# Second layer's norm from sums taken before the residual add, ten row tiles held for the second tokens, and DVE's order tied through both chains

## The chip, the cores and the metric

The kernel runs on one core of a Trainium2 chip. The metric is device microseconds (us) for one execution. Engines are named as in the profile: PE is TensorE's matmul (PEld its weight load), DVE is VectorE, ACT is ScalarE, POOL is GpSimd, SP is SyncE, whose queue issues most of the DMAs.

## The reference

The kernel computes two layers over 256 tokens of width 2048. In each, the input is normed, modulated, projected by one wide weight matrix, sent through four attention branches and a gate, projected back, normed again and added to the input:

```
def rmsnorm(x, g):
    y = x * rsqrt(mean(x * x, axis=-1) + 1e-6)
    return y * g

for li in range(2):
    shift, scale, gate = split(silu(c) @ w_ada[li] + b_ada[li], 3)
    h = rmsnorm(x, g_pre[li]) * (1 + scale) + shift
    p = split_columns(h @ w_in[li])
    ...                                   # four branches, each 512 wide
    mixed = concat(branches) * silu(p["gate"])
    y = mixed @ w_out[li]
    x = x + gate * rmsnorm(y, g_post[li])
```

What matters here is the seam between the layers: `rmsnorm(y)` and the add give x, and the second layer's `rmsnorm(x, g_pre[1])` needs the sum of squares of each row of that new x. With r the reciprocal root of y's mean square and u = y * gate * g_post, the new row is x + r * u, and its sum of squares can also be had as sum(x^2) + r * sum(2*u*x) + r^2 * sum(u^2).

## The kernel before, in words

All of it is one function, `trunk`, with nested helpers; the instructions are written in program order, and a planner puts them in order on each engine when the kernel is built. The planner goes by a model of durations and gives a free engine the earliest instruction in program order among those that the model says are ready. On the chip each engine then follows that fixed order. `with tc.issue_after(ins)` keeps the instructions in it behind `ins` on their engine; it sets an order and waits for no data.

Tokens are two tiles t of 128 rows (T = 2), the width is 16 tiles kt of 128 (KT), and weights come two kt at a time (a unit k2). Products are made of two parts per operand: `split` (L297) has ACT round a weight unit to `whi` (L300) and DVE subtract for `wlo` (L301), and notes that subtraction as `ada.behind`; `mm3` (L318) issues three matmuls, L320 to L322. `weights` (L304) loads a unit on SP's queue (L310), splits it, and after every second unit calls `ada.run`, which sums weights of the modulation vectors that were loaded before (L143 on DVE, one pass over 128x1024 each with an accumulated output) and loads further ones (L133).

`tok_major` (L333) is a projection with tokens as rows. With `late` set, the last `late` of the 16 kt are multiplied for t = 0 only, held, and multiplied for t = 1 at the end, so that the result of t = 0 is ready earlier. Held units must keep their split weights: the last three have buffers of their own (`own`, L948 to L954), others stay in the three rotating pairs `whi`/`wlo` of the pool splp (L73).

The output projection (L943) has four column parts n of 512. For each and each t, ACT squares the result with an accumulated sum (L960) and DVE multiplies it by the gate row into `yg` (L961). In the last part (n = 3, late = 6) there follows, per t: the sum of the four parts (L966), mean and epsilon (L96), the power -1/2 on POOL (L97), four updates of x in place on DVE (L971), in the last layer four output DMAs (L973). In the first layer `norm_row` (L394) then squares the new x on ACT in four pieces (L399), sums (L401), takes L96 and L97 again, and `rms_row` scales the identity by the result (L429), has PE multiply it with ones (L431) to lay it out as a row, and ACT copies it to `rrow` (L432). x goes to DRAM (L979). Before the second token tile's `norm_row`, `turned` (L434) is written, in which PE transposes x for the first three units (L440).

The second layer begins with `ada.until(1, 3)` (L826), which has the outstanding L143 sums done up to its fourth unit, and with `modulated` (L443): per kt, DVE multiplies the transposed x by gain and `rrow` (L454), ACT adds the shift and rounds (L456), DVE takes the rest (L457). Then the first projections, `latent` (L369), split their weights and run.

x itself is loaded for the residual at L937, after the buffers of the mixed branches come free. `wk` is a rotating pool of four scratch tiles, `bank()` one of four PSUM banks.

Of the kernel before, what the change touches and what calls it, by code (L numbers as in the profile page):

```python
# [20 lines left out]
P = 128  # L21
D = 2048
# [31 lines left out]
LATE = 6  # L54
# [7 lines left out]
def trunk(ctx: ExitStack, tc: tile.TileContext, a):  # L62
# [31 lines left out]
    def rsqrt_mean(out, ssq, n, w):  # L94
        ms = small.tile([P, 8], F32, name="ms")
        nc.vector.tensor_scalar(ms[:, :w], ssq, 1.0 / n, EPS, op0=ALU.mult, op1=ALU.add)  # L96
        nc.gpsimd.tensor_tensor(out, ms[:, :w], mhalf[:, :w], op=ALU.pow)  # L97

# [23 lines left out]
    class Ada:  # L122
# [60 lines left out]
        def finish(self, L, li, u):  # L183
# [4 lines left out]
            else:  # L188

                h, j = (u - K2) // 2, (u - K2) % 2  # L190
                if j == 0:
                    self.gate = small.tile([P, 32], F32, name="gcol", bufs=2)
                    nc.gpsimd.memset(self.gate, 0.0)
# [4 lines left out]
                if j == 1:  # L198

                    turn = small.tile([P, 32], F32, name="grow", bufs=2)  # L200
                    nc.vector.transpose(turn, self.gate)
                    L.row[h] = row = dram.tile([8, 4, 32], F32, name=f"row{li}{h}")
                    for q in range(4):
                        nc.gpsimd.dma_start(row[:, q, :], turn[32 * q:32 * q + 8, :])
# [89 lines left out]
    def bank():  # L294
        return psm.tile([P, 512], F32, name="main")
# [98 lines left out]
    def norm_row(L, t):  # L394

        ssp = small.tile([P, 4], F32, name="ssp")
        jk = bank()
        for h in range(4):
            nc.scalar.activation(jk, L.cols(t, 512 * h, 512), AF.Square, accum_out=ssp[:, h:h + 1])  # L399
        ss = small.tile([P, 1], F32, name="ss")  # L400
        nc.vector.tensor_reduce(ss, ssp, axis=AX.X, op=ALU.add)  # L401
        rms_row(L, t, ss)

# [19 lines left out]
    def rms_row(L, t, ss):  # L423
        rstd = small.tile([P, 1], F32, name="rstd")
        rsqrt_mean(rstd, ss, D, 1)
        if t == 0:
            L.rrow = lay.tile([P, S], F32, name="rrow")
        dg = work.tile([P, 512], F32, name="wk")[:, 0:P]
        nc.vector.tensor_scalar(dg, ident, rstd, None, op0=ALU.mult)  # L429
        rp = bank()[:, 0:P]  # L430
        nc.tensor.matmul(rp, ones, dg, start=True, stop=True)  # L431
        nc.scalar.copy(L.rrow[:, t * P:(t + 1) * P], rp)  # L432

# [388 lines left out]
    def layer(li):  # L822
# [118 lines left out]
        ssy = small.tile([P, T, 4], F32, name="ssy", bufs=1)  # L941
        ygs = []
        for n in range(4):  # L943
# [14 lines left out]
            for t in range(T):  # L958
                jk = work.tile([P, 512], F32, name="wk")
                nc.scalar.activation(jk, ps[t], AF.Square, accum_out=ssy[:, t, n:n + 1])  # L960
                nc.vector.tensor_mul(yg[:, t, :], ps[t], gg[n // 2][:, 512 * (n % 2):512 * (n % 2) + 512])  # L961
                if n < 3:
                    continue
                ss = small.tile([P, 1], F32, name="ss")
                rstd = small.tile([P, 1], F32, name="rstd")
                nc.vector.tensor_reduce(ss, ssy[:, t, :], axis=AX.X, op=ALU.add)  # L966
                rsqrt_mean(rstd, ss, D, 1)
                for m in range(4):
                    cs = slice(512 * m, 512 * (m + 1))
                    xs = x[t][m // 2][:, 512 * (m % 2):512 * (m % 2) + 512]  # L970
                    nc.vector.scalar_tensor_tensor(xs, ygs[m][:, t, :], rstd, xs, op0=ALU.mult, op1=ALU.add)  # L971
                    if last:
                        nc.sync.dma_start(a["out"][t * P:(t + 1) * P, cs], xs)  # L973
                if not last:
                    if t == 1:
                        layers[li + 1].tp = [turned(layers[li + 1], k2) for k2 in range(3)]
                    norm_row(layers[li + 1], t)
# [113 lines left out]
```

## Time and profile before

| what | us |
|---|---|
| median of 3 runs | 1119.47 (1119.19 to 1120.66) |
| the profiled execution | 1120.7 |
| its span in the profile | 1118.9 |
| PE busy (matmul) | 1073.8 |
| DVE busy | 876.2 |
| ACT busy | 558.2 |
| POOL busy | 50.1 |

The span is the time between the first and the last instruction of the profiled execution; 1.8 us lie around it. Busy times of the engines overlap each other. Matmuls are pipelined, so that a matmul's listed duration is longer than the distance to the next one.

### The profile page before, as it was taken

The numbers are of one execution on the slowest core, as the hardware profiler recorded it, in microseconds if no ns is written. First come the engines' busy times: TensorE is split into PE (matmuls) and PEld (weight loads), VectorE is DVE, ScalarE is ACT, GpSimd is POOL, SyncE is SP. The second block draws the span as 40 slices with busy tenths as digits, with TensorE's granted clock in tenths as the row PEclk, the third lists the DMA queues.
The fourth block names the chain that finished last, engine by engine and source line by source line (L and its number), as shares of the span: only waits on it lengthen the run. The fifth ranks groups of instructions, "written<-read, shape, count | busy, mean of one in ns | idle before, by whom it ended". The sixth has DMA issues, their size and how long they took to land.

```text
span 1118.9 us, 19443 instructions
## 1 busy us (share of the span) xinstructions
PE 1073.8 (96%) x7562; PEld 991.2 (89%) x7562; DVE 876.2 (78%) x1470; ACT 558.2 (50%) x929; POOL 50.1 (4%) x70
## 2 busy tenths in 40 slices
PE   3899999999999999999959999999999999999996
PEld 2798989999899999988749999999999899998885
DVE  4598897999999778887778887989997655556463
ACT  3455344345454766654444554554554476645451
POOL 1000000000003000000000000000112000000000
PEclk9899999999999999999979999999999999999999
DMA  9998998988677677899867999867687765357541
GB/s 366 348 330 306 354 341 260 346 276 278 236 231 244 212 246 251 280 359 310 304 273 263 367 339 325 294 219 229 205 273 254 258 196 166 132 189 263 188 151 75
DMA packets 83308, 294.75 MB, mean 263 GB/s; under 512 B 9768, under 2 KB 10048, under 8 KB 83088
## 3 DMA queue, kind: packets, MB, share of 16 engines
q1 hardware_dynamic: 81216, 288.36, 74.5%
q0 software_dynamic: 1856, 5.09, 1.3%
q8 instruction: 59, 0.97, 0.4%
q14 instruction: 33, 0.27, 0.1%
q10 hardware_dynamic: 144, 0.07, 0.0%
HBM read 289.25 MB, written 4.23 MB: 262 GB/s over the span
## 4 chain that ended last, share of the span: by engine, by line
PE 89%; DVE 5%; DMA 3%; issue 1%; ACT 1%; SPq 0%; POOL 0%; DVEq 0%; POOLq 0%; ACTq 0%
PE main L322 27%; PE main L320 27%; PE main L321 27%; PE att L511 1%; DVE raw L143 1%; DMA raw<-in_w_g_dram 1%; PE att L670 1%; DVE wlo L301 1%; DMA raw<-in_w_ada_dram 1%; PE att L704 1%; PE att L484 1%; PE att L528 1%; DVE big L971 1%; ACT main L399 1%; PE att L737 0%
## 5 line engine op out<-in xcount | busy, mean ns | idle before, releaser
L300 ACT CAST whi<-raw 128x1024 fp32r<-128x1024 f32 (+2 forms) x340 | 349.2, 1028 | 407.7 <-PE main L321 164.9
L301 DVE TENSOR_TENSOR wlo<-raw,whi 128x1024 fp32r<-128x1024 f32 (+2 forms) x340 | 404.8, 1194 | 168.8 <-ACT whi L300 165.9
L321 PE MATMUL main<-act_lo,whi 128*128 128x256 f32 x1568 | 440.9, 283 | 0.0
L320 PE MATMUL main<-act_hi,whi 128*128 128x256 f32 x1568 | 440.3, 283 | 0.0
L322 PE MATMUL main<-act_hi,wlo 128*128 128x256 f32 x1568 | 433.0, 284 | 1.9 <-DVE wlo L301 1.8
L321 PEld LDWEIGHTS main<-act_lo,whi 128*128 128x128 f32 x1568 | 295.9, 189 | 3.0 <-issue 2.0
L320 PEld LDWEIGHTS main<-act_hi,whi 128*128 128x128 f32 x1568 | 295.9, 189 | 2.7 <-issue 0.9
L322 PEld LDWEIGHTS main<-act_hi,wlo 128*128 128x128 f32 x1568 | 290.8, 189 | 4.5 <-DVE wlo L301 2.9
L143 DVE SCALAR_TENSOR_TENSOR raw<-raw,scb 128x1024 f32<-128x1024 f32 x176 | 211.8, 1224 | 0.0
L321 PE MATMUL main<-wlo,act_hi 128*128 128x512 f32 (+2 forms) x552 | 210.4, 383 | 0.1
L322 PE MATMUL main<-whi,act_lo 128*128 128x512 f32 (+2 forms) x552 | 207.8, 381 | 1.0 <-DVE act_lo L457 1.0
L320 PE MATMUL main<-whi,act_hi 128*128 128x512 f32 (+2 forms) x552 | 193.0, 384 | 7.3 <-ACT act_hi L456 7.3
L320 PEld LDWEIGHTS main<-whi,act_hi 128*128 128x128 f32 x552 | 104.7, 192 | 26.6 <-ACT act_hi L456 7.8
L322 PEld LDWEIGHTS main<-whi,act_lo 128*128 128x128 f32 x552 | 105.3, 192 | 20.7 <-DVE act_lo L457 1.3
L321 PEld LDWEIGHTS main<-wlo,act_hi 128*128 128x128 f32 x552 | 105.9, 192 | 19.9 <-DVE wlo L301 0.8
L97 POOL TENSOR_TENSOR rstd<-ms,mhalf 128x1 f32<-128x1 f32 (+1 forms) x12 | 8.1, 677 | 569.9 <-DVE ms L96 477.8
L476 ACT ACTIVATE lat_acc<-lat_acc,mx 128x256 f32<-128x256 f32 (+1 forms) x56 | 25.3, 453 | 7.2 <-DVE mx L474 7.2
L692 POOL TENSOR_TENSOR cbuf<-strip,cbuf 128x128 f32<-128x128 f32 (+1 forms) x16 | 18.2, 1166 | 193.3 <-DVE cbuf L690 108.2
L150 PE MATMUL ada_ps<-raw,strip 128*32 128x128 f32 x256 | 10.9, 326 | 14.7 <-DMA raw<-in_w_ada_dram 14.6
L678 DVE SCALAR_TENSOR_TENSOR cbuf<-wk,wid,cbuf 128x128 f32<-128x128 f32 (+1 forms) x64 | 23.6, 411 | 1.0 <-ACT wk L675 0.9
L150 PEld LDWEIGHTS ada_ps<-raw,strip 128*32 128x32 f32 x256 | 8.2, 130 | 16.0 <-DVE on L412 14.6
L675 ACT ACTIVATE wk<-att 128x256 f32<-128x256 f32 (+1 forms) x32 | 14.9, 488 | 10.5 <-PE att L670 6.6
(206 smaller groups left out, 880.9 us busy)
## 6 DMA issues: line engine op xcount, KB each, us to landing
raw<-in_w_g_dram SPq DMA_DIRECT2D x240, 512.0 KB, 5.4
raw<-in_w_ada_dram SPq DMA_DIRECT2D x192, 512.0 KB, 5.4
raw<-in_w_out_dram SPq DMA_DIRECT2D x64, 512.0 KB, 4.8
raw<-in_w_g_dram SPq DMA_DIRECT2D x16, 400.0 KB, 5.5
raw<-in_w_g_dram SPq DMA_DIRECT2D x16, 384.0 KB, 4.6
raw<-in_w_uq_dram SPq DMA_DIRECT2D x6, 384.0 KB, 3.9
big<-in_xt_dram SPq DMA_DIRECT2D x4, 512.0 KB, 8.0
raw<-in_w_ukv_dram SPq DMA_DIRECT2D x4, 512.0 KB, 4.3
```

The source lines that it names most:

```text
L143: nc.vector.scalar_tensor_tensor(w, w, 0.5, scb[:, 1024 * (n % 2):1024 * (n % 2 + 1)], op0=ALU.mult, op1=ALU.mult, accum_out=self.part[:, ...
L150: nc.tensor.matmul(self.ps[32 * q:32 * q + 32, 0:n], lhs, w[:, n * q:n * (q + 1)], start=not self.started, stop=last, tile_position=(0, 32 ...
L300: nc.scalar.copy(hi, src)
L301: ada.behind = nc.vector.tensor_sub(lo, src, hi).ins
L320: nc.tensor.matmul(out, sh, mh, start=first, stop=False, **kw)
L321: nc.tensor.matmul(out, sh, ml, start=False, stop=False, **kw)
L322: nc.tensor.matmul(out, sl, mh, start=False, stop=last, **kw)
L399: nc.scalar.activation(jk, L.cols(t, 512 * h, 512), AF.Square, accum_out=ssp[:, h:h + 1])
L476: nc.scalar.activation(lg[:, i, :], lg[:, i, :], AF.Exp, bias=mx[:, i:i + 1], accum_out=sm[:, i:i + 1])
L675: nc.scalar.activation(rl[:, 0:2 * sw], dp[:, 0:2 * sw], AF.Relu)
L678: nc.vector.scalar_tensor_tensor(sc[t], rl[:, u * sw:(u + 1) * sw], wid[:, t, h:h + 1], sc[t], op0=ALU.mult, op1=ALU.add)
L692: nc.gpsimd.tensor_add(L.cb[t][:, h, :], strip_of(4 + h, 1, t)[:, 0, :], s)
```

## The change

The sum of squares of the new x is no longer taken from the new x. ACT squares the old x in eight pieces after its load, and squares `yg` after each eviction; DVE multiplies 2 * yg by x with an accumulated sum. From these three sums per token tile and the reciprocal root, small DVE instructions give the new sum of squares, while the updates of x run separately. `LATE` goes from 6 to 10, in both layers. In the first layer the order on DVE of both token tiles' chains is written out with `issue_after`: evict t = 0, its output norm, its input norm, two updates, evict t = 1, its output norm, the other two updates of t = 0, the input norm of t = 1, the two row layouts and the updates of t = 1 between them. The transposes come last. `norm_row` goes; `row_of` is the end of `rms_row`. Two small tiles, `gcol` and `grow`, get one buffer instead of two.

```diff
-LATE = 6
+LATE = 10
...
     def rsqrt_mean(out, ssq, n, w):
         ms = small.tile([P, 8], F32, name="ms")
-        nc.vector.tensor_scalar(ms[:, :w], ssq, 1.0 / n, EPS, op0=ALU.mult, op1=ALU.add)
+        done = nc.vector.tensor_scalar(ms[:, :w], ssq, 1.0 / n, EPS, op0=ALU.mult, op1=ALU.add)
         nc.gpsimd.tensor_tensor(out, ms[:, :w], mhalf[:, :w], op=ALU.pow)
+        return done.ins
...
-                    self.gate = small.tile([P, 32], F32, name="gcol", bufs=2)
+                    self.gate = small.tile([P, 32], F32, name="gcol", bufs=1)
...
-                    turn = small.tile([P, 32], F32, name="grow", bufs=2)
+                    turn = small.tile([P, 32], F32, name="grow", bufs=1)
...
-    def norm_row(L, t):
...
     def rms_row(L, t, ss):
         rstd = small.tile([P, 1], F32, name="rstd")
         rsqrt_mean(rstd, ss, D, 1)
+        row_of(L, t, rstd)
+
+    def row_of(L, t, rstd):
...
-        nc.vector.tensor_scalar(dg, ident, rstd, None, op0=ALU.mult)
+        done = nc.vector.tensor_scalar(dg, ident, rstd, None, op0=ALU.mult)
...
+        return done.ins
...
-        ssy = small.tile([P, T, 4], F32, name="ssy", bufs=1)
+        sums = small.tile([P, T, 4, 4], F32, name="sums", bufs=1)
+        if not last:
+            for t in range(T):
+                for n in range(4):
+                    jk = work.tile([P, 512], F32, name="wk")
+                    nc.scalar.activation(jk, x[t][n // 2][:, 512 * (n % 2):512 * (n % 2) + 512], AF.Square,
+                                         accum_out=sums[:, t, 1, n:n + 1])
...
+            def evict(t, behind):
                 jk = work.tile([P, 512], F32, name="wk")
-                nc.scalar.activation(jk, ps[t], AF.Square, accum_out=ssy[:, t, n:n + 1])
-                nc.vector.tensor_mul(yg[:, t, :], ps[t], gg[n // 2][...])
+                nc.scalar.activation(jk, ps[t], AF.Square, accum_out=sums[:, t, 0, n:n + 1])
+                with tc.issue_after(behind):
+                    nc.vector.tensor_mul(yg[:, t, :], ps[t], gg[n // 2][...])
+                if not last:
+                    jk = work.tile([P, 512], F32, name="wk")
+                    nc.scalar.activation(jk, yg[:, t, :], AF.Square, accum_out=sums[:, t, 2, n:n + 1])
+                    jk = work.tile([P, 512], F32, name="wk")
+                    nc.vector.scalar_tensor_tensor(jk, yg[:, t, :], 2.0, part(t, n), op0=ALU.mult, op1=ALU.mult,
+                                                   accum_out=sums[:, t, 3, n:n + 1])
+
+            def output_norm(t, behind):
+                ...
+                with tc.issue_after(behind):
+                    nc.vector.tensor_reduce(ss[:, 0:1], sums[:, t, 0, :], axis=AX.X, op=ALU.add)
+                return ss, rstd, rsqrt_mean(rstd, ss[:, 0:1], D, 1)
+
+            def input_norm(t, ss, rstd):
+                nc.vector.tensor_reduce(ss[:, 1:4], sums[:, t, 1:4, :], axis=AX.X, op=ALU.add)
+                sn = small.tile([P, 1], F32, name="sn", bufs=2)
+                nc.vector.scalar_tensor_tensor(sn, ss[:, 2:3], rstd, ss[:, 3:4], op0=ALU.mult, op1=ALU.add)
+                nc.vector.scalar_tensor_tensor(sn, sn, rstd, ss[:, 1:2], op0=ALU.mult, op1=ALU.add)
+                nc.vector.tensor_scalar(sn, sn, 0.0, None, op0=ALU.max)
+                rstd2 = small.tile([P, 1], F32, name="rstd2", bufs=2)
+                return rstd2, rsqrt_mean(rstd2, sn, D, 1)
+
+            def updated(t, ms, rstd, behind):
+                for m in ms:
+                    with tc.issue_after(behind):
+                        behind = nc.vector.scalar_tensor_tensor(part(t, m), ygs[m][:, t, :], rstd, part(t, m),
+                                                                op0=ALU.mult, op1=ALU.add).ins
+                return behind
+
+            if n < 3:
+                for t in range(T):
+                    evict(t, ada.behind)
+            elif last:
+                ...                       # per t: evict, output_norm, then update and output DMA by parts
+            else:
+                N = layers[li + 1]
+                evict(0, ada.behind)
+                ss0, r0, done = output_norm(0, ada.behind)
+                row0, done = input_norm(0, ss0, r0)
+                done = updated(0, (0, 1), r0, done)
+                evict(1, done)
+                ss1, r1, done = output_norm(1, done)
+                updated(0, (2, 3), r0, done)
+                row1, done = input_norm(1, ss1, r1)
+                with tc.issue_after(done):
+                    done = row_of(N, 0, row0)
+                done = updated(1, (0, 1), r1, done)
+                with tc.issue_after(done):
+                    done = row_of(N, 1, row1)
+                updated(1, (2, 3), r1, done)
+                N.tp = [turned(N, k2) for k2 in range(3)]
+                for t in range(T):
                     for h in range(2):
                         nc.sync.dma_start(x_dram[...], x[t][h])
```

## Rows read from the trace of the kernel before

**Rows 1.** The page, part 4: what the chain of work that ended last is made of.
```profile
PE 89%; DVE 5%; DMA 3%; issue 1%; ACT 1%; SPq 0%; POOL 0%; DVEq 0%; POOLq 0%; ACTq 0%
```

**Rows 2.** Busy time by stretches at the seam: us from the span's start, its length, then busy us (and count) of PE, PEld, DVE, ACT, POOL, granted TensorE clock, DMA share, GB/s.
```profile
551.78:569.00 17.22, 17.12 (x73) 13.27 (x72) 17.22 (x27) 6.93 (x9) 0.00 (x0) 1.00 0.97 348
569.00:583.48 14.48, 4.16 (x16) 2.76 (x16) 8.20 (x24) 6.89 (x20) 2.21 (x4) 0.63 0.68 275
585.00:590.00 5.00, 5.00 (x22) 4.98 (x21) 4.87 (x13) 2.41 (x6) 0.00 (x0) 0.53 0.00 0
```

**Rows 3.** Timeline of PE at the end of the first layer's last output part: start us, us, what. Units lat_acc/cbuf, lat_hi/lat_lo and idx are the three held ones.
```profile
562.20 0.39 PE L320 MATMUL main<-lat_acc,act_hi 128*128 128x512 f32 x1
...
563.34 0.40 PE L321 MATMUL main<-lat_lo,act_hi 128*128 128x512 f32 x1
...
565.63 0.39 PE L322 MATMUL main<-idx,act_lo 128*128 128x512 f32 x1
...
568.58 0.39 PE L322 MATMUL main<-idx,act_lo 128*128 128x512 f32 x1
```

**Rows 4.** Timeline of ACT in the same stretch: start us, us, what, and in brackets the idle time before it with what ended it.
```profile
550.69 1.05 ACT L300 CAST lat_acc<-raw 128x1024 fp32r<-128x1024 f32 x1 [2.63 <-DMA raw<-in_w_out_dram]
...
563.15 1.85 ACT L300 CAST whi<-raw 128x800 fp32r<-128x800 f32 x2 [7.59 <-DMA raw<-in_w_g_dram]
566.35 0.84 ACT L300 CAST whi<-raw 128x768 fp32r<-128x768 f32 x1 [1.35 <-DMA raw<-in_w_g_dram]
567.09 0.59 ACT L960 ACTIVATE wk<-main 128x512 f32<-128x512 f32 x1
```

**Rows 5.** Timeline of DVE at the seam. Between the two L143 rows lie three more of the same kind, five in all.
```profile
559.82 1.22 DVE L143 SCALAR_TENSOR_TENSOR raw<-raw,scb 128x1024 f32<-128x1024 f32 x1
...
564.40 1.22 DVE L143 SCALAR_TENSOR_TENSOR raw<-raw,scb 128x1024 f32<-128x1024 f32 x1
...
565.55 0.98 DVE L301 TENSOR_TENSOR wlo<-raw,whi 128x800 fp32r<-128x800 f32 x1
...
567.77 0.95 DVE L301 TENSOR_TENSOR wlo<-raw,whi 128x768 fp32r<-128x768 f32 x1
568.64 0.68 DVE L961 TENSOR_TENSOR v<-main,k 128x512 f32<-128x512 f32 x1
...
569.30 0.14 DVE L177 TENSOR_TENSOR shift<-parts,sml 128x2 f32<-128x2 f32 x1
569.37 0.15 DVE L179 SCALAR_TENSOR_TENSOR gain<-parts,sml 128x2 f32<-128x2 f32 x1
...
575.40 0.68 DVE L961 TENSOR_TENSOR v<-main,k 128x512 f32<-128x512 f32 x1
576.01 0.15 DVE L966 TENSOR_REDUCE ss<-ssy 128x1 f32<-128x4 f32 x1
576.19 0.15 DVE L96 TENSOR_SCALAR ms<-ss 128x1 f32<-128x1 f32 x1
577.07 0.75 DVE L971 SCALAR_TENSOR_TENSOR big<-v,rstd,big 128x512 f32<-128x512 f32 x1 [0.73 <-POOL rstd L97]
577.74 0.74 DVE L971 SCALAR_TENSOR_TENSOR big<-q,rstd,big 128x512 f32<-128x512 f32 x1
...
581.94 0.29 DVE L429 TENSOR_SCALAR wk<-cst,rstd 128x128 f32<-128x128 f32 x1 [0.73 <-POOL rstd L97]
583.48 2.44 DVE L454 SCALAR_TENSOR_TENSOR wk<-att,gain,rrow 128x256 f32<-128x256 f32 x6 [1.25 <-ACT rrow L432]
```

**Rows 6.** Busy time by single microseconds, columns as in Rows 2: the granted clock as it falls and as it comes back.
```profile
573.00:574.00 1.00, 0.00 (x0) 0.00 (x0) 0.06 (x1) 0.97 (x5) 0.00 (x0) 0.50 1.02 418
...
589.00:590.00 1.00, 1.00 (x6) 1.00 (x5) 0.87 (x3) 0.00 (x0) 0.00 (x0) 0.65 0.00 0
```

**Rows 7.** The output projection of the first layer: an eviction on DVE's timeline with the two weight splits behind it, and on PEld's timeline the one wait of this stage.
```profile
525.75 1.28 DVE L961 TENSOR_TENSOR q<-main,q 128x512 f32<-128x512 f32 x2
526.95 2.35 DVE L301 TENSOR_TENSOR wlo<-raw,whi 128x1024 fp32r<-128x1024 f32 x2
...
555.33 0.19 PEld L321 LDWEIGHTS main<-wlo,act_hi 128*128 128x128 f32 x1 [0.50 <-DVE wlo L301]
```

**Rows 8.** Line 937, the loads of x: count, durations of issue, first and last start; and the time from issue to landing.
```profile
L937 SPq DMA_DIRECT2D big<-in_x_dram x4: 327/328/328, 471.0 to 492.3; - x4
...
DMA to landing us min/median/max: 5.0/5.6/7.6
```

**Rows 9.** The page, part 5: the sums of the modulation weights, two SBUF inputs and an accumulated output.
```profile
L143 DVE SCALAR_TENSOR_TENSOR raw<-raw,scb 128x1024 f32<-128x1024 f32 x176 | 211.8, 1224 | 0.0
```

**Rows 10.** Timelines of ACT and DVE at the end of the kernel (second layer).
```profile
1106.03 0.60 ACT L960 ACTIVATE wk<-main 128x512 f32<-128x512 f32 x1 [11.48 <-PE main L322]
1110.15 0.60 ACT L960 ACTIVATE wk<-main 128x512 f32<-128x512 f32 x1 [3.43 <-PE main L322]
...
1106.75 0.69 DVE L961 TENSOR_TENSOR v<-main,k 128x512 f32<-128x512 f32 x1 [10.94 <-ACT wk L960]
1111.10 0.68 DVE L961 TENSOR_TENSOR v<-main,k 128x512 f32<-128x512 f32 x1
```

**Rows 11.** The queues: SP's timeline with the writes of x between the layers, and from the page, part 6, the small gate rows on POOL's queue (KB each, us to landing).
```profile
571.76 8.39 SPq L979 DMA_DIRECT2D x_mid<-big  x4
...
row<-grow POOLq DMA_DIRECT2D x16, 1.0 KB, 3.9
```

More of the change, by code (lines that the diff above doesn't have):

```diff
@@ L392, in put @@
                 nc.scalar.copy(d, ps[t][:, :w])
-    def norm_row(L, t):
[L396 to L402, printed above, removed]
     def norm_rows_of_turned(L):
@@ L957, in layer, with part @@
             ygs.append(yg)
-            for t in range(T):
+            def part(t, m):
+                return x[t][m // 2][:, 512 * (m % 2):512 * (m % 2) + 512]
+            def evict(t, behind):
                 jk = work.tile([P, 512], F32, name="wk")
-                nc.scalar.activation(jk, ps[t], AF.Square, accum_out=ssy[:, t, n:n + 1])
[L961 to L964, printed above, removed]
-                rstd = small.tile([P, 1], F32, name="rstd")
[L966 to L977, printed above, removed]
@@ new lines, in evict @@
+                nc.scalar.activation(jk, ps[t], AF.Square, accum_out=sums[:, t, 0, n:n + 1])
+                with tc.issue_after(behind):
+                    nc.vector.tensor_mul(yg[:, t, :], ps[t], gg[n // 2][:, 512 * (n % 2):512 * (n % 2) + 512])
+                if not last:
[4 more added lines that the diff above has]
+                                                   accum_out=sums[:, t, 3, n:n + 1])
@@ new lines, in output_norm @@
+            def output_norm(t, behind):
+                ss = small.tile([P, 4], F32, name="ss")
+                rstd = small.tile([P, 1], F32, name="rstd")
+                with tc.issue_after(behind):
[9 more added lines that the diff above has]
+                return rstd2, rsqrt_mean(rstd2, sn, D, 1)
@@ new lines, in updated @@
+            def updated(t, ms, rstd, behind):
[9 more added lines that the diff above has]
+                for t in range(T):
+                    evict(t, ada.behind)
+                    ss, rstd, done = output_norm(t, ada.behind)
+                    for m in range(4):
+                        done = updated(t, [m], rstd, done)
+                        nc.sync.dma_start(a["out"][t * P:(t + 1) * P, 512 * m:512 * (m + 1)], part(t, m))
+            else:
[15 more added lines that the diff above has]
+                N.tp = [turned(N, k2) for k2 in range(3)]
+                for t in range(T):
```

## The prediction

> **What bounds the kernel now.** First the chain of waits: PE makes up 89% of it [rows 1], so the kernel is bound by matmuls nearly everywhere, and a change outside PE can gain only where PE stands still. The busy time by stretches shows the one long standstill besides the start: from 569.00 to 583.48 PE works 4.16 of 14.48 us [rows 2]. That is the seam between the layers. PE's timeline says where it begins: the last output matmul of the first tokens starts at 565.63, that of the second at 568.58 [rows 3], so PE is done at about 568.97 (568.58 + 0.39). DVE's timeline says where it ends: the first `modulated` instruction, L454, starts at 583.48 [rows 5]. Between them both token tiles go one after the other through the chain square, multiply, norm, four updates, four squares, norm, row layout. DVE is full before that (17.22 of 17.22 us) and has gaps after (8.20 of 14.48) [rows 2]; idle between 551.78 and 583.48 is thus 6.28 us. It is full because five L143 sums and three weight splits of the next layer run while the first tokens' result lies ready: their multiply starts only at 568.64, behind the third split at 567.77 [rows 5], which waited for ACT's rounding at 566.35, which waited for a DMA [rows 4].
>
> **Part 1, the late tiles.** From 565.63 to 568.58 thirteen matmuls of the second tokens are issued, so one takes 2.95 / 13 = 0.227 us [rows 3]. Ten held tiles make 30 matmuls: the first tokens' last matmul would start at 568.58 - 30 x 0.227 = 561.8 and be done at 562.2, against 565.63 + 0.39 = 566.0 now. PE's own work is the same. What it could cost is an order that runs dry: tile pairs four to eight must be split sooner, and one wait of 0.50 us for a split is there already [rows 7]. Bounds: nothing, if the planner fills in second-token matmuls as it does now (562.20 lies ahead of 563.34 [rows 3]), or one L143 in front of a split, 1.1 us. I take 0.2.
>
> **Part 2, the added sums.** In the first layer ACT gets eight squares of x and eight of `yg`, DVE eight multiplications with accumulation. A square is 0.6 us plus a short read of the sum, 0.7 (1106.03 to 1106.75) [rows 10]. A DVE pass over 128x512 with two SBUF inputs takes 0.67 from start to start (577.07 to 577.74) [rows 5]; L143, of the same kind with an accumulated output, takes 1.224 for twice the columns [rows 9], so accumulation adds nothing visible, and I take 0.67. The Trainium skill (Vector Engine (DVE) Microarchitecture Reference, Points that are easy to get wrong) says that this instruction form with two non-bf16 SBUF sources runs at half throughput for want of a port to the accumulator; doubled, the two at the seam would add 1.3 us, and L143's 1.224 us for 1024 columns speaks against a doubling.
> Six of the eight lie in the first three output parts. There DVE has 1.3 us more per eviction, ahead of two splits (526.95) [rows 7] that PE wants a few microseconds later. Bounds: nothing, or the whole excess shows three times, 4 us; since the only wait of the stage is 0.50, I take 0.1 each, 0.3. The last of these evictions lies just ahead of the full stretch; of its 1.3 us I let 0.3 run over into that. ACT has room: 6.93 of 17.22 us busy [rows 2]. The squares of x wait for loads that land 5.0 to 7.6 us after issue [rows 8]; casts queue behind them. Between nothing and the third rival below I take 0.1.
>
> **Part 3, the seam.** Gone are the eight squares of the new x and with them DVE's waits for them. Added on DVE are two multiplications (1.33) and, per token tile, three more small instructions (two STTs and a maximum), 0.18 each where one needs the other's result (576.01 to 576.19) [rows 5]. A mean to its first use is 0.88 through POOL (576.19 to 577.07) [rows 5].
> *If only dependencies count:* 568.97, square 0.7, multiply 0.61 (575.40 to 576.01), the product 0.67, sum and mean 0.36, two updates of the first tokens 1.33 (they cover POOL's power), five small ones 0.9, row layout 0.2, two updates 1.33: the second row layout is at 575.07. From it to L454 it is 1.54 now (581.94 to 583.48) [rows 5], and the last two updates fit in it: L454 at 576.6, 6.9 earlier.
> *If DVE's work counts:* the 6.28 us of idle time shrink by 1.33 + 1.1 and 0.3 to 3.6; were none left, L454 would come at 579.9, 3.6 earlier.
> I take a course between, nearest to the rows: the five L143 stay in front as now, for their data arrive while the second tokens run, to 565.55, and one split with them, to 566.45 [rows 5]. Then multiply and product 1.28, sum and mean 0.36, reaching 568.1; power to 568.8, while a second split runs to 569.0; five small ones to 569.9; two updates 571.2; multiply and product of the second tokens 572.5; sum and mean 572.8; two updates 574.2; five small ones 575.1; row layout and two updates 576.6; L454 at 578.1. With 0.3 from the earlier eviction and 0.3 of the third split, 578.7: a gain of 4.8. After L454 another 0.3 is given back where that split lies among the modulated tiles. What is late next is DVE itself, not ACT or POOL.
> The chain has dependent small instructions at 0.18 where unrelated ones are 0.07 apart (569.30, 569.37) [rows 5]. The Trainium skill (VectorE: DVE Perf Modes, The DRAIN you can't avoid) states that a semaphore between chained DVE operations costs nothing extra; at 0.07 the chains would be about 1.1 shorter, and the rows show the 0.18.
>
> **Part 4, the rest.** At the kernel's end the first tokens come 2.7 us (12 x 0.227) sooner. The second tokens' square starts at 1110.15 and its multiply now at 1111.10, behind the first tokens' updates; freed, it follows the square as 1106.75 follows 1106.03, at 1110.87: 0.2 gained [rows 10]. `issue_after` at other places orders what data order already. The writes of x to DRAM are written after all updates; SP spends 571.76 to 580.15 on them now [rows 11] and would issue them from about 574 to 579, and no load of the next layer is wanted before. `gcol` and `grow` with one buffer: the second use comes 16 L143 later, over 16 x 1.1 us, the rows land in 3.9 [rows 11]: nothing.
>
> **Sum.** -4.8 + 0.3 - 0.2 + 0.2 + 0.3 + 0.1 = -4.1 us. On the profiled execution (1120.7, span 1118.9) that is 1116.6; the median of the runs, 1119.47, lies 0.1% lower, so 1115.4.
>
> **Rivals.**
> *Dependencies alone.* The planner puts the first tokens' chain ahead of the L143 sums, since it is earlier in program order than the second layer's. For: 562.2 lies before 563.15, ACT's next cast [rows 4]. Against: in the planner's model loads seem to arrive early; ACT stood 2.63 us for a DMA at 550.69 [rows 4], so casts and sums are placed soon. Gain 6.9 + 0.2 - 0.6 = 6.5: 1113.0. The clock could add to it: it is at 0.50 from 573 and back only in 589 to 590 [rows 6], with PE fully busy at 0.53 in the 5 us from 585 [rows 2]; if transposes and first matmuls lie closer together, some 1 to 1.5 us of that come back: 1111.5.
> *DVE's holes stay.* The ties order the chain but the other work still lies in it, and POOL's powers leave holes, so that little more than the two waits for squares (2 x 1.06) goes, less the added 0.6 of Part 1 and 2 and with the 0.2 at the end: about -1.7, 1117.8. For it: DVE is full to 569 in any case.
> *Slower: ACT is held by the squares of x.* They stand ahead of the output part's casts. Where the planner believes a load to be there early, ACT stops for it: the hold of 2.63 at 550.69 [rows 4] went with the wait of 0.50 on PE [rows 7], so some 2.1 are covered. A hold of a whole landing, 5.6 [rows 8], costs 3.5; two of the four loads make 7.0: 1115.4 + 7.0 = 1122.4. It decides once PE idles over 6.3 us (4.1 + 2.2) between 471 and 505. Against: the loads are issued over 21 us, most of them long before their squares need run.
> *The tie does not do what it says:* it sets an order only, and no urgency; then it is the second rival.
>
> **How the numbers follow.** The forecast's own case, 1113.5 to 1117.2, has 0.47; dependencies alone 0.15; DVE's holes 0.24; ACT held 0.10; other losses, as a new order of the whole second layer, 0.04. A measurement of this kernel tells some 0.2% (2.2 us) from no change, so faster means below 1117.2: 0.47 + 0.15 + 0.08 of the holes = 0.70; same 0.16; slower 0.14. The range takes in dependencies with the clock, 1111.5, and reaches over the holes to no change, 1119.8.
>
> **What would show it.** Right: the first tokens' last output matmul about 6.8 us ahead of the second's; no ACT square between the updates and L454; DVE without idle time from the multiply to L454, and that about 9 to 10 us after PE's last output matmul instead of 14.5; PE as busy as now from 480 to 560. Wrong: L143 or L301 rows inside the second tokens' chain, PE waits for `whi` or `wlo` between 470 and 560, a first multiply that still starts after 568, or another PE total in the second layer.

## The result, and the profile after

The changed kernel takes 1113.73 us (1113.09 to 1114.45, 4 runs) where the kernel before takes 1120.07 (1119.19 to 1121.77, 4 runs): a ratio of 0.995, 95% interval 0.9937 to 0.9963, or 6.3 us less. The forecast was 4.1 us less. The total came out on the forecast's side and within its range, but from other places: by the medians of e1 and e2 below, some 2.1 to 2.4 us of it come from the change's work, and 3.6 to 3.9 from something that the prediction had put at nothing, the place of the weight buffers in memory. The profiled execution of the changed kernel took 1114.45 us (span 1112.7).

In the code of after the lines have moved: split copies L301/L302, main matmuls L321 to L323, modulation sums L144, evictions L966 (square), L968 (multiply), L971 (square of `yg`), L973 (product with x), small norm steps L980 to L989, updates L996, row layout L423, `modulated` L449.

From the page: busy time, and the chain that ended last, beside [rows 1]. PE is 5.2 us less busy (1073.8 before) with the same number of instructions.

```profile
PE 1068.6 (96%) x7562; PEld 985.5 (89%) x7562; DVE 881.3 (79%) x1492; ACT 562.3 (51%) x945; POOL 50.9 (5%) x70
...
PE 90%; DVE 5%; DMA 3%; issue 1%; ACT 0%; SPq 0%; DVEq 0%; POOLq 0%; POOL 0%; ACTq 0%
```

The seam by stretches, columns as in [rows 2]: from PE's last output matmul (its end, 567.34) to the first `modulated` instruction.

```profile
550.00:567.34 17.34, 16.92 (x72) 12.92 (x70) 17.34 (x28) 8.80 (x15) 0.00 (x0) 1.00 0.93 333
567.34:579.27 11.93, 3.95 (x16) 2.88 (x16) 11.11 (x35) 2.56 (x8) 3.09 (x4) 0.70 0.72 285
```

The standstill is 11.93 us long; in the terms of the prediction it was 583.48 - 568.97 = 14.51. So 2.6 are gained here. The reader should see DVE: full before the seam as it was, and now also in it, 11.11 of 11.93 where it had 8.20 of 14.48.

PE's timeline, beside [rows 3]: the last output matmuls of the first and of the second tokens.

```profile
564.23 0.39 PE L323 MATMUL main<-idx,act_lo 128*128 128x512 f32 x1
...
566.95 0.39 PE L323 MATMUL main<-idx,act_lo 128*128 128x512 f32 x1
```

They are 2.72 us apart, not the 6.8 forecast. ACT's timeline, beside [rows 4]:

```profile
548.90 1.05 ACT L301 CAST lat_acc<-raw 128x1024 fp32r<-128x1024 f32 x1 [3.54 <-DMA raw<-in_w_out_dram]
...
561.36 0.87 ACT L301 CAST whi<-raw 128x800 fp32r<-128x800 f32 x1 [5.30 <-DMA raw<-in_w_g_dram]
562.56 0.86 ACT L301 CAST whi<-raw 128x800 fp32r<-128x800 f32 x1 [0.33 <-DMA raw<-in_w_g_dram]
565.32 0.84 ACT L301 CAST whi<-raw 128x768 fp32r<-128x768 f32 x1 [1.90 <-DMA raw<-in_w_g_dram]
566.06 0.59 ACT L966 ACTIVATE wk<-main 128x512 f32<-128x512 f32 x1
```

The first tokens' square stands behind a cast that waits for a DMA: their result is there at 564.62 (564.23 + 0.39), the square starts at 566.06. DVE's timeline, beside [rows 5]:

```profile
558.63 1.21 DVE L144 SCALAR_TENSOR_TENSOR raw<-raw,scb 128x1024 f32<-128x1024 f32 x1
...
562.06 0.68 DVE L973 SCALAR_TENSOR_TENSOR wk<-k,big 128x512 f32<-128x512 f32 x1
...
563.82 1.21 DVE L144 SCALAR_TENSOR_TENSOR raw<-raw,scb 128x1024 f32<-128x1024 f32 x1
564.97 1.88 DVE L302 TENSOR_TENSOR wlo<-raw,whi 128x800 fp32r<-128x800 f32 x2
566.78 0.41 DVE L647 COPY cbuf<-cst 128x128 f32<-128x128 f32 x2
567.11 0.94 DVE L302 TENSOR_TENSOR wlo<-raw,whi 128x768 fp32r<-128x768 f32 x1
567.98 0.68 DVE L968 TENSOR_TENSOR v<-main,k 128x512 f32<-128x512 f32 x1
...
570.14 0.22 DVE L987 SCALAR_TENSOR_TENSOR sn<-ss,rstd 128x1 f32<-128x1 f32 x1 [0.34 <-POOL rstd L97]
570.39 0.22 DVE L988 SCALAR_TENSOR_TENSOR sn<-sn,rstd,ss 128x1 f32<-128x1 f32 x1
...
572.23 0.68 DVE L968 TENSOR_TENSOR v<-main,k 128x512 f32<-128x512 f32 x1
...
579.27 2.44 DVE L449 SCALAR_TENSOR_TENSOR wk<-att,gain,rrow 128x256 f32<-128x256 f32 x6 [0.18 <-ACT rrow L426]
```

All five L144, one L973, all three splits and two copies (L647) still stand ahead of the first multiply; from it to L449 DVE has two holes with a releaser, 0.34 and 0.18. Between 480 and 567 PEld waits twice, beside [rows 7]:

```profile
553.54 0.19 PEld L322 LDWEIGHTS main<-wlo,act_hi 128*128 128x128 f32 x1 [0.85 <-DVE wlo L302]
556.48 0.19 PEld L322 LDWEIGHTS main<-wlo,act_hi 128*128 128x128 f32 x1 [0.32 <-DVE wlo L302]
```

And the end of the kernel, ACT and then DVE, beside [rows 10]: the second tokens' multiply follows its square by 0.72 (it was 0.95).

```profile
1104.15 0.60 ACT L966 ACTIVATE wk<-main 128x512 f32<-128x512 f32 x1 [4.61 <-PE main L323]
...
1104.87 0.69 DVE L968 TENSOR_TENSOR v<-main,k 128x512 f32<-128x512 f32 x1 [0.86 <-ACT wk L966]
```

### The profile page after: what moved, and what is told of

Same layout as the page of the kernel before. It is cut to its first block, busy times and chain, and to the rows that moved or that the text cites. A ratio compares the mean times of both kernels' runs of the same rounds, so it can differ in the third digit from the quotient of the medians.

```text
span 1112.7 us, 19474 instructions
## 1 busy us (share of the span) xinstructions
PE 1068.6 (96%) x7562; PEld 985.5 (89%) x7562; DVE 881.3 (79%) x1492; ACT 562.3 (51%) x945; POOL 50.9 (5%) x70
## 4 chain that ended last, share of the span: by engine, by line
PE 90%; DVE 5%; DMA 3%; issue 1%; ACT 0%; SPq 0%; DVEq 0%; POOLq 0%; POOL 0%; ACTq 0%
PE main L323 27%; PE main L322 27%; PE main L321 27%; PE att L506 1%; DMA raw<-in_w_g_dram 1%; DVE wlo L302 1%; PE att L665 1%; DVE raw L144 1%; DMA raw<-in_w_ada_dram 1%; PE att L699 1%; PE att L479 1%; PE att L523 1%; PE att L732 0%; PE att L631 0%; PE att L632 0%
## 5 line engine op out<-in xcount | busy, mean ns | idle before, releaser
L301 ACT CAST whi<-raw 128x1024 fp32r<-128x1024 f32 (+2 forms) x340 | 349.1, 1027 | 398.7 <-PE main L322 157.9
L302 DVE TENSOR_TENSOR wlo<-raw,whi 128x1024 fp32r<-128x1024 f32 (+2 forms) x340 | 404.8, 1194 | 163.7 <-ACT whi L301 160.8
L321 PE MATMUL main<-act_hi,whi 128*128 128x256 f32 x1568 | 438.1, 282 | 0.0
L323 PE MATMUL main<-act_hi,wlo 128*128 128x256 f32 x1568 | 430.6, 282 | 2.5 <-DVE wlo L302 2.5
L321 PEld LDWEIGHTS main<-act_hi,whi 128*128 128x128 f32 x1568 | 294.7, 188 | 2.7 <-issue 0.9
L323 PEld LDWEIGHTS main<-act_hi,wlo 128*128 128x128 f32 x1568 | 289.4, 188 | 5.1 <-DVE wlo L302 3.6
L144 DVE SCALAR_TENSOR_TENSOR raw<-raw,scb 128x1024 f32<-128x1024 f32 x176 | 211.9, 1224 | 0.0
L323 PE MATMUL main<-whi,act_lo 128*128 128x512 f32 (+2 forms) x552 | 207.6, 381 | 1.1 <-DVE act_lo L452 1.1
L321 PE MATMUL main<-whi,act_hi 128*128 128x512 f32 (+2 forms) x552 | 191.7, 381 | 7.5 <-ACT act_hi L451 7.5
L321 PEld LDWEIGHTS main<-whi,act_hi 128*128 128x128 f32 x552 | 104.2, 191 | 27.4 <-ACT act_hi L451 8.0
L323 PEld LDWEIGHTS main<-whi,act_lo 128*128 128x128 f32 x552 | 105.0, 191 | 20.8 <-DVE act_lo L452 1.9
```

Source lines behind the costliest of these rows:

```text
L144: nc.vector.scalar_tensor_tensor(w, w, 0.5, scb[:, 1024 * (n % 2):1024 * (n % 2 + 1)], op0=ALU.mult, op1=ALU.mult, accum_out=self.part[:, ...
L301: nc.scalar.copy(hi, src)
L302: ada.behind = nc.vector.tensor_sub(lo, src, hi).ins
L321: nc.tensor.matmul(out, sh, mh, start=first, stop=False, **kw)
L323: nc.tensor.matmul(out, sl, mh, start=False, stop=last, **kw)
```

## Experiments: where 3.9 us came from that are not at the seam

Set side by side, the two traces part long before the seam: from the start to PE's last output matmul after has gained 1.63 us in small steps, and in the second layer it gains some 2 more, though until the output projection the order of instructions on PE, DVE and ACT is the same. What differs is one matmul from the next: the mean distance between the starts of two 256-column matmuls of the same kind (600 to 830 us, 1271 and 1290 distances; the few above 0.2 us, where the next such row is missing or another instruction lies between, are left out) is 118.36 ns before and 117.22 after. Grouped by shape, three lines have 1568 of these each, so 1 ns is worth at most 4.7 us. Of the change only the memory layout reaches that far: the small tiles lie below the raw weight buffers and the split buffers (`whi`, `wlo`), and with fewer bytes of small tiles (`gcol` and `grow` with one buffer, other sums) both start 160 bytes lower; `whi` starts at 204480 instead of 204640.

**e1: before, in the layout of after.**

```diff
-self.gate = small.tile([P, 32], F32, name="gcol", bufs=2)     # and grow
+self.gate = small.tile([P, 32], F32, name="gcol", bufs=1)     # and grow
-ssy = small.tile([P, T, 4], F32, name="ssy", bufs=1)
+ssy = small.tile([P, 32], F32, name="ssy", bufs=1)[:, 0:4 * T].rearrange("p (t n) -> p t n", t=T)
```

> The kernel before with nothing of the change but its memory layout: gcol and grow with one buffer and the sums tile padded to 128 bytes, so that the weight and split buffers behind the small tiles lie 160 bytes lower, as in the changed kernel. Theory A (layout): of the 6.3 us between the two kernels some 4 come from a faster pace of the 256-column matmuls (117.4 ns from start to start against 118.4), and that pace hangs on where the buffers lie; then this kernel has the pace 117.4 and is about 4 us faster than the kernel before, near 1116. Theory B (the pace is a matter of the run, or of the code itself): pace 118.4 and no change, within 1 us.

Measured 1115.82 us (before 1119.68 in the same comparison), ratio 0.9969 [0.9957, 0.9981]: 3.9 us from the layout alone by the medians (3.5 by the ratio), the seam nearly unchanged (14.2 us for 14.5).

**e2: after, in the layout of before.**

```diff
-sums = small.tile([P, T, 4, 4], F32, name="sums", bufs=1)
+sums = small.tile([P, 72], F32, name="sums", bufs=1)[:, 0:16 * T].rearrange("p (t k n) -> p t k n", t=T, k=4)
```

> The changed kernel with its sums tile padded by 160 bytes, so that the weight and split buffers lie where they lay before; the order of every engine is the same as in the changed kernel. Theory A (layout): pace 118.4 ns, and only the seam's gain is left, about 2 us under the kernel before, near 1118. Theory B: as the changed kernel, about 6.3 us under the kernel before, near 1114.

Measured 1117.31, ratio 0.9979 [0.997, 0.9987]: the change without the new place is worth 2.4 us, and its seam is 11.93 us as in after.

**e5, e9, e10, e12: which buffers, and by what rule.** Each is the kernel before with a pad between pools, which POOL clears once (left out below); e10 has the edit of e1 too.

```diff
 e5:  +gap = pool("gap"); gap.tile([P, 8], F32)     # 32 bytes between rawp and splp
 e9:  +gap = pool("gap"); gap.tile([P, 8], F32)     # 32 bytes ahead of rawp
 e10: +gap = pool("gap"); gap.tile([P, 40], F32)    # 160 bytes between rawp and splp, with e1's edit
 e12: +gap = pool("gap"); gap.tile([P, 24], F32)    # 96 bytes between rawp and splp
```

> The kernel before with 32 bytes of padding between the raw weight buffers and the split buffers: the raw buffers stay where they are, the split buffers start at 204672 instead of 204640, a multiple of 64 bytes as in the changed kernel, but further up instead of further down. Nothing else changes. If the alignment of the split operands sets the pace of the matmuls (A1): 117.4 ns from start to start instead of 118.4 and about 3.9 us less, 1115.8. If it is the address of the raw buffers, of another tile or the distance moved (A2): 118.4 ns and 1119.7.

> The kernel before with the raw weight buffers and the split buffers both 32 bytes higher (171904 and 204672), so that both start at multiples of 64 bytes, as they do in the changed kernel 160 bytes lower. Nothing else changes. If it is the raw buffers' start, or both together, at a multiple of 64 bytes (A3): 117.4 ns from one 256-column matmul to the next and 1115.8, as in e1. If it is something of the exact place (A4): 118.4 to 119 ns and 1119.7 to 1121.7.

> The kernel before with the raw weight buffers 160 bytes lower (171712), where the changed kernel has them, and the split buffers where they were (204640). If the raw buffers' place alone sets the pace (A3, raw): 117.4 ns and 1115.8. If both must move (A3, both): 118.4 ns or more and 1119.7 or more.

> The kernel before with the split buffers 96 bytes higher, at 204736; the raw buffers stay. So far the split buffers' start went with the distance between two 256-column matmuls: 204480 with 117.4 ns, 204640 with 118.4, 204672 with 118.8. 204736 lies 256 bytes above 204480. If the place within 256 bytes sets the pace (A5): 117.4 ns and 1115.8. If not (A6, a longer period, or the distance to other buffers): 118 ns or more and 1118 to 1122, and the rule stays open.

| kernel | raw from | `whi` from | ns per 256-column matmul, 600 to 830 us | us | ratio to before |
|---|---|---|---|---|---|
| before | 171872 | 204640 | 118.36 | 1119.7 to 1120.1 | 1 |
| e10 | 171712 | 204640 | 118.35 | 1119.22 | 0.9998 [0.9989, 1.0006] |
| e2 (the change) | 171872 | 204640 | 118.37 | 1117.31 | 0.9979 [0.997, 0.9987] |
| e5 | 171872 | 204672 | 118.85 | 1121.72 | 1.0018 [1.001, 1.0027] |
| e9 | 171904 | 204672 | 118.85 | 1122.70 | 1.0026 [1.0015, 1.0037] |
| e1 | 171712 | 204480 | 117.38 | 1115.82 | 0.9969 [0.9957, 0.9981] |
| e12 | 171872 | 204736 | 117.35 | 1116.75 | 0.9973 [0.9962, 0.9984] |
| after (the change) | 171712 | 204480 | 117.22 | 1113.73 | 0.995 [0.9937, 0.9963] |

The profile shows it in plain counts: busy time of 600 to 830 us, columns as in [rows 2], where PE is busy throughout; the count behind PE's time is how many matmuls it got through. In order: before, after, e2, e1, e5, e10. Where the second layer starts earlier, as in e2 and after, other matmuls fall into this stretch too, so e2 has 7 more than before at the same pace.

```profile
600.00:830.00 230.00, 230.00 (x1683) 216.59 (x1682) 205.12 (x372) 118.32 (x192) 10.90 (x11) 1.00 0.83 288
```

```profile
600.00:830.00 230.00, 230.00 (x1703) 216.64 (x1702) 205.70 (x376) 119.22 (x192) 10.96 (x12) 1.00 0.83 288
```

```profile
600.00:830.00 230.00, 230.00 (x1690) 216.62 (x1689) 205.59 (x377) 117.57 (x190) 10.96 (x12) 1.00 0.83 288
```

```profile
600.00:830.00 230.00, 230.00 (x1701) 216.71 (x1700) 206.62 (x379) 117.90 (x191) 11.99 (x12) 1.00 0.83 288
```

```profile
600.00:830.00 230.00, 230.00 (x1680) 216.82 (x1679) 204.88 (x372) 117.50 (x192) 11.67 (x11) 1.00 0.82 287
```

```profile
600.00:830.00 230.00, 230.00 (x1684) 216.59 (x1684) 205.28 (x373) 118.09 (x192) 10.94 (x12) 1.00 0.82 288
```

A stretch of the first layer, ahead of all of the change's own work, has no such shift: before and after. There e1 has 1307 as after, e12 1306, and e2, e5, e9 and e10 have 1299 to 1301 as before.

```profile
150.00:330.00 180.00, 179.93 (x1300) 168.10 (x1300) 168.70 (x295) 85.30 (x130) 1.42 (x2) 1.00 0.82 278
```

```profile
150.00:330.00 180.00, 179.63 (x1307) 167.69 (x1306) 169.53 (x298) 85.43 (x131) 1.41 (x2) 1.00 0.82 278
```

My first rule, a start at a multiple of 64 bytes (A1), fell with e5: 204672 is one, and it is the slowest. The raw buffers don't matter: e10 moves them and nothing follows, e9 moves them too and has e5's pace. The place of the split buffers (`whi` and `wlo` move together) sets the pace: 204736, 256 bytes above 204480, has the same pace as that (e12), as A5 expects. That it repeats every 256 bytes isn't shown by one pair.

## Experiments: the seam

**e3: after with six held tiles; e4: before with ten.**

```diff
 e3: -LATE = 10   +LATE = 6
 e4: -LATE = 6    +LATE = 10
```

> The changed kernel with six held row tiles instead of ten. If the ten tiles do what the prediction says, the first tokens' result comes 2.7 us later and the second layer starts 1 to 2.7 us later: about 1115.5. Rival: the first tokens' square stands on ACT behind a rounding of the next layer's weights that waits for a DMA, in either case until about 1 us before the last output matmul, so the four tiles more bring nothing at the seam (within 0.5 us), and without the wait for splits in the output projection this kernel may be 0.5 us faster: 1113 to 1114.

> The kernel before with ten held tiles instead of six and nothing else. Prediction's step: the first tokens' result 2.7 us earlier, at most that much gained at the seam and 0.2 at the end. Rival as for the other one: the first tokens' chain still starts behind the DMA-bound rounding, so nothing is gained at the seam and 0 to 0.7 lost to splits that come late: 1119.5 to 1121.

e3: 1113.47 us, ratio 0.9947 [0.9935, 0.9959], as after. e4: 1119.46, ratio 1.0001 [0.9993, 1.001], as before. Ten tiles bring nothing in either that the intervals, some 1 us each way, can tell. PE's timeline of e3, the same two matmuls as above:

```profile
563.98 0.39 PE L323 MATMUL main<-idx,act_lo 128*128 128x512 f32 x1
...
566.70 0.39 PE L323 MATMUL main<-idx,act_lo 128*128 128x512 f32 x1
```

2.72 us apart, as with ten; before and e4 have 2.95 both (e4: 564.59 and 567.54). The number of held tiles doesn't set the lead: whatever is held, the planner puts the second tokens' matmuls of all but the last two units (`lat_hi`/`lat_lo` and `idx`) between the first tokens', and twelve (2.72 / 0.227) remain behind. DVE's timeline of e3 shows what stands in front of the chain:

```profile
564.72 1.89 DVE L302 TENSOR_TENSOR wlo<-raw,whi 128x800 fp32r<-128x800 f32 x2
...
566.86 0.95 DVE L302 TENSOR_TENSOR wlo<-raw,whi 128x768 fp32r<-128x768 f32 x1
567.73 0.69 DVE L968 TENSOR_TENSOR v<-main,k 128x512 f32<-128x512 f32 x1
```

**e6: the three splits of the next layer behind the chain's start.**

```diff
+if held_back:                         # the next layer's first three splits
+    on_act, on_dve = held_back.pop()
+    with tc.issue_after(on_act): nc.scalar.copy(hi, src)
+    with tc.issue_after(on_dve): ada.behind = nc.vector.tensor_sub(lo, src, hi).ins
...
-evict(0, ada.behind)
+held_back.extend([evict(0, ada.behind)] * 3)      # its square on ACT, its product on DVE
```

> The changed kernel with the next layer's first three splits tied behind the first tokens' square (on ACT) and product (on DVE), so that they run in the chain's own gaps and not ahead of it. Theory (DVE's work bounds the seam; from 564.97 on it has hardly a hole, so an order changes nothing): the first multiply starts at about 565, 3 us earlier, and the first modulated tile starts where it does now, at 578.7 to 579.3; 1113.2 to 1113.7. Rival (the chain's start bounds the seam): the 3 us come through, the first modulated tile at about 576.5, 1111.

1114.92 us (1112.0 to 1115.64), ratio 0.9948 [0.9936, 0.996]: no difference from after. DVE's timeline of e6 (the lines have moved by nine: L977 multiply, L308 the splits, L458 `modulated`):

```profile
565.11 0.69 DVE L977 TENSOR_TENSOR v<-main,k 128x512 f32<-128x512 f32 x1
...
566.47 0.98 DVE L308 TENSOR_TENSOR wlo<-raw,whi 128x800 fp32r<-128x800 f32 x1
...
567.57 1.85 DVE L308 TENSOR_TENSOR wlo<-raw,whi 128x800 fp32r<-128x800 f32 x2
...
578.75 2.44 DVE L458 SCALAR_TENSOR_TENSOR wk<-att,gain,rrow 128x256 f32<-128x256 f32 x6 [0.18 <-ACT rrow L435]
```

The multiply comes 2.87 us earlier (565.11 for 567.98), `modulated` 0.52 (578.75 for 579.27): the splits now take their time inside the chain, which is 13.64 us long instead of 11.29. The theory held: the amount of DVE's work sets the end of the seam, not the chain's start. Only the median lies 1.2 us above the expected range, with runs on both sides of it.

**e7: two modulation sums fewer ahead of the seam.**

```diff
-PACE = {..., "out": 1.25, "next": 1}
+PACE = {..., "out": 1.5, "next": 1}
```

> The changed kernel with 1.5 instead of 1.25 modulation sums asked for per pair of units in the output projection, so that three of the sums of 1.15 us lie ahead of the seam's splits instead of five. Theory (DVE's work bounds the seam): two sums less are 2.3 us, of which the third split gives back some; the first modulated tile at about 577.5 and 1112.0. Rival (DMA bounds that stage, whose share is 0.97 already): the output projection's weights come later, PE waits more for wlo than the 1.2 us now, and the time is 1114 to 1116.

1110.87 us (1110.36 to 1112.33), ratio 0.992 [0.9908, 0.9932]: 2.9 less than after, the fastest kernel of this study. DVE's timeline of e7:

```profile
561.50 1.22 DVE L144 SCALAR_TENSOR_TENSOR raw<-raw,scb 128x1024 f32<-128x1024 f32 x1
...
566.64 0.69 DVE L968 TENSOR_TENSOR v<-main,k 128x512 f32<-128x512 f32 x1 [0.69 <-ACT wk L966]
...
577.93 2.44 DVE L449 SCALAR_TENSOR_TENSOR wk<-att,gain,rrow 128x256 f32<-128x256 f32 x6 [0.18 <-ACT rrow L426]
```

Now DVE waits for the square, which waits for PE, and the seam is 577.93 - 567.01 = 10.92 us, 1.0 less. The two waits of 0.85 and 0.32 for `wlo` are gone too. The profiled execution of e7, the slowest of its five, is 2.1 shorter than that of after: it reaches the output projection 0.5 later (476.97 for 476.45), gains 0.9 there and 1.0 at the seam, and 0.8 behind the seam. Most of the last goes with the clock. Below is the busy time of the second four microseconds after the first `modulated` instruction, in after, in e7 and in e2, columns as in [rows 2]. In the four before these, all three have the lower of TensorE's two levels (a granted clock of 0.50, 1.2 GHz) with PE busy for 2.97 or 2.98 of them; in these PE is busy throughout, and the granted clock is 0.67 on average in after and already 0.95 in e7, so that 21 and 27 matmuls run. But e2, whose seam is as long as after's, has 0.92 and 26: the clock's return differs without e7's edit too, so this part can't be put down to it. What makes up the medians' 2.9 beyond the projection and the seam stays open.

```profile
583.27:587.27 4.00, 4.00 (x21) 3.99 (x21) 2.40 (x7) 0.97 (x3) 0.00 (x0) 0.67 0.00 0
```

```profile
581.93:585.93 4.00, 4.00 (x27) 4.00 (x27) 2.62 (x8) 1.74 (x3) 0.00 (x0) 0.95 0.01 2
```

```profile
584.67:588.67 4.00, 4.00 (x26) 4.00 (x25) 2.51 (x8) 1.74 (x3) 0.00 (x0) 0.92 0.00 0
```

**e8: after without the ties along the chains.**

```diff
-done = updated(0, (0, 1), r0, done)
-evict(1, done)
...
+updated(0, (0, 1), r0, first)         # first: the last split ahead of the chain
+evict(1, first)
...
-with tc.issue_after(done):
-    done = row_of(N, 0, row0)
+row_of(N, 0, row0)
```

> The changed kernel without the ties along the two chains: every instruction of them is only tied behind the last split before the first tokens' multiply, and the planner orders the rest. It puts the small steps of the second layout behind all updates. Theory (the ties are what keeps the second layout's steps ahead of the updates): up to 2 us later than now at the first modulated tile, 580.5 to 581.3, and 1115 to 1115.8. Rival (DVE's work is the same in any order): 579.3 and 1113.7.

1116.74 us, ratio 0.9969 [0.9957, 0.9981], by the medians 3.0 more than after, whose interval it just overlaps. DVE's timeline of e8: a small step of the second layout stands behind the last update, and the chain goes on through POOL, PE and ACT from there.

```profile
578.82 0.74 DVE L996 SCALAR_TENSOR_TENSOR big<-v,rstd,big 128x512 f32<-128x512 f32 x1
579.49 0.21 DVE L988 SCALAR_TENSOR_TENSOR sn<-sn,rstd,ss 128x1 f32<-128x1 f32 x1
...
582.21 2.44 DVE L449 SCALAR_TENSOR_TENSOR wk<-att,gain,rrow 128x256 f32<-128x256 f32 x6 [1.19 <-ACT rrow L426]
```

So without the ties `modulated` is 2.9 us later, of which 0.8 was there before the seam (PE's last output matmul ends at 568.16, in after at 567.34). The seam is 582.21 - 568.16 = 14.05 us long, 2.1 more than in after, and the new sums alone gain little: it was 14.51 before. The expectation's mechanism held at the seam, with its "up to 2 us"; start and time lie beyond its ranges. Whether an order written out would gain as much in the kernel before, with the old norm, no run tries.

**e11: before, in the layout of after, with e7's edit.**

> The kernel of e1 (before, in the changed kernel's layout) with 1.5 instead of 1.25 modulation sums asked for per pair of units in the output projection; nothing of the change. Theory (DVE's work ahead of the seam bounds either kernel): DVE is full up to the first tokens' multiply there as well, so the sums that leave are gained as in e7, some 2.5 to 3 us: 1113. Rival (in the kernel before, the waits between the chains bound the seam, and the first tokens' result is there only at 566): half of that at most, 1114.5 to 1115.8; then the change is what makes the sums' place worth something.

1115.31 us (1113.07 to 1115.92), ratio 0.9959 [0.9946, 0.9971], against e1's 0.9969 [0.9957, 0.9981]: in time no difference can be told, and the median lies in the rival's range. The profiled run, the fastest of six, shows one at the seam: DVE's timeline of e11,

```profile
564.05 0.69 DVE L961 TENSOR_TENSOR v<-main,k 128x512 f32<-128x512 f32 x1 [0.57 <-ACT wk L960]
...
578.64 2.44 DVE L454 SCALAR_TENSOR_TENSOR wk<-att,gain,rrow 128x256 f32<-128x256 f32 x6 [1.25 <-ACT rrow L432]
```

both 2.07 us earlier than in e1, whose rows are

```profile
566.12 0.69 DVE L961 TENSOR_TENSOR v<-main,k 128x512 f32<-128x512 f32 x1
...
580.71 2.44 DVE L454 SCALAR_TENSOR_TENSOR wk<-att,gain,rrow 128x256 f32<-128x256 f32 x6 [1.25 <-ACT rrow L432]
```

with the chain between them 14.59 us in both. Of the 2.07, 0.41 was there before the output projection began (475.29 for 475.70). The new chain takes 11.29 in after and in e7. How much of the rest the runs keep stays open.

## Why the prediction was right in total and wrong in its terms

**The bound.** Right: PE nearly everywhere, and one standstill. What bounds that standstill after the change is DVE, as the prediction said would come next; e6 and e7 show it. Two of the prediction's signs of being wrong came as well: waits for `wlo` (0.85 and 0.32), and another PE total in the second layer (523.8 us busy from the first `modulated` instruction on, for 525.6), which is the layout's.

**Late tiles.** The step "ten held tiles make 30 matmuls" failed. It took all held tiles to stay behind the first tokens' last matmul, though the prediction knew that the planner fills in. The lead stayed at 2.72 us (e3), and what it would have cost, 0.2, can't be told from the added sums' share: PEld waits 1.2 in all after, 1.1 in e3, 0.9 in e1 and e4, 0.50 before.

**Added sums.** The product took 0.683 us (median of L973), forecast 0.67. The Trainium skill (Vector Engine (DVE) Microarchitecture Reference, Points that are easy to get wrong) has this form at half throughput with two non-bf16 SBUF sources; the trace does not agree, since the plain multiply L968, one of whose sources is PSUM, takes 0.68 as well. The squares of x on ACT waited for a load once, 0.28 us, and no wait of PE came of it: the third rival did not occur. Of the last early eviction 0.3 us was let run into the full stretch; its L973 lay there whole (562.06).

**The seam.** Forecast 4.8, measured 2.6. The course that was forecast failed at its start: one split ahead of the first multiply and the result at 562.2, so that it starts 2.52 us before PE ends (566.45 against 568.97). It starts 0.64 after PE ends (567.98 against 567.34), behind all three splits: 3.2 us later. The chain itself was better than forecast, 11.29 us from multiply to `modulated` against 12.25, since the splits were no longer in it; within it the dependent small steps stood 0.25 apart (570.14 to 570.39), not 0.18. 3.2 less 1.0 is the 2.2 that lack. But the start is where they show and not why: in e6 the multiply starts 1.91 us before PE ends (565.11 against 567.02), and its seam of 11.73 is only 0.2 shorter. Counted on DVE, whose work sets the end, the forecast has the five sums done 3.42 us before PE's end (565.55 against 568.97) and 13.15 us from there to `modulated`; after has 2.37 (564.97 against 567.34) and 14.30, so 1.05 and 1.15 are lost. In the first lies the last early product whole, of which 0.3 was counted; in the second the whole third split, of which 0.3 was counted, and two copies (L647) of 0.33 together, which no term has. The remainder is not taken apart by any run. The bound "if DVE's work counts", 3.6, was the nearest of the three numbers, and was itself too high by the extra L973 and those steps and holes. "Dependencies alone" fell with e6. "DVE's holes stay" has nearly the time of e2 (1117.8 and 1117.31) but not the mechanism: of 11.93 us 0.82 are idle.

**The tie.** That it does nothing was a rival; e8 shows that it is worth 2.1 us of the 2.6 gained at the seam.

**The end.** Right: 0.2 forecast; from PE's last matmul to the last update it was 5.05 us (1109.72 to 1114.77) and is 4.83 (1103.72 to 1108.55).

**`gcol` and `grow`: "nothing".** The largest failed term. The wait that was costed there did not come, but the bytes, with those of the larger sums tile, moved the split buffers: 3.9 us by e1, 3.6 by e2 against after (by the ratios 3.5 and 3.2).

**Sum.** By its measured terms the change's work is -2.6 at the seam, -0.2 at the end and +0.7 of waits in the output projection (1.17 for 0.50): -2.1. Measured: -2.4 (e2 to before), -2.1 (after to e1). With the layout's 3.6 to 3.9 that makes 5.7 to 6.3 of the 6.3. So the forecast of 4.1 was near by two errors of opposite sign, and that is luck: in the layout of before (e2) the change takes 1117.31, just outside the forecast's own case of 1113.5 to 1117.2.

## What to carry to other kernels

Where an engine is full up to the start of a chain, starting the chain earlier gains nothing; count that engine's work in front of the seam and move work of no urgency away from it, which in the changed kernel was worth 2.9 us (e7), while in the kernel before no gain can be told (e11). Before an edit's gain is put down to its idea, run the edit's memory layout alone: a few bytes of small tiles moved a PE-bound kernel by some 0.3%. An order that a planner chooses has to be read from the new trace; a parameter like `LATE` says what may be late, not what is.

## What the runs showed of the hardware that was not expected

The pace of 256-column fp32r matmuls goes with the place of the buffers from which their weights are loaded: 117.4 ns with `whi` at 204480 or 204736, 118.4 at 204640, 118.85 at 204672; it did not change with other buffers' places. The 512-column matmuls of the output projection, which stream the split buffers as moving operand, kept 233.3 ns at either place (before and after); at 204672 (e5, e9) they took 232.4, a little less, where the 256-column ones are slowest. The two good places are 256 bytes apart; whether 128 would do, whether `whi` or `wlo` or both decide, and what in the chip makes it so, was not tried and stays open.
